# Up projection of 28 expert blocks moved beside the routing and the gate matrix of a PEER layer, activations parked in HBM

## The chip, the cores and the metric

The kernel runs on one core of a Trainium2 chip. The metric is the device time of one execution in microseconds; the time before is the median of three runs.

## What is computed

The reference is one layer of a bidirectional encoder on 512 tokens of width 2048 in fp32: RMSNorm, an input projection, attention in one head group and a gated linear recurrence in the other, an output projection, and then the part that matters here, a PEER channel mixer over 128 x 128 single-neuron experts, and a final RMSNorm. The mixer, cut to its core:

```python
q = (xt @ w_pq).reshape(T, 8, 2, 128)
s1, s2 = q[:, :, 0] @ sub_k1, q[:, :, 1] @ sub_k2      # per head
v1, i1 = top_k(s1, 16);  v2, i2 = top_k(s2, 16)
cand = v1[..., :, None] + v2[..., None, :]             # 256 per head
sc, sel = top_k(cand, 16);  eidx = (i1 * 128 + i2)[sel]
gates = softmax(sc)
out = sum over the 128 chosen e of  gates * gelu(x . u_emb[e]) * v_emb[e]
```

Each token chooses 8 x 16 = 128 of 16384 experts.

## The kernel before

Tokens 160 to 511 (352 of them, TD) are computed densely: all 16384 experts, as 128 blocks of 128 experts, with a gate matrix that is zero where an expert was not chosen. The first 160 tokens are computed sparsely: for each chosen slot a row of u_emb and of v_emb is gathered by an indirect DMA. Both run at the same time in the main loop.

All fp32 products on TensorE are made of three matmuls in a reduced format: an operand is split into `hi` (a cast on ScalarE, L171) and `lo` (raw minus hi, on VectorE, L183), and hi x hi, hi x lo, lo x hi are summed. Weights come in 1 MB tiles, `raw`, two buffers, in the order of a list of sources; `take` splits one tile ahead, and the load of tile i + 2 stands behind the split of tile i on SyncE's queue. So each unit of work on TensorE needs one `hi` on ScalarE and one `lo` on VectorE, made while the unit before it runs.

The stages that the change touches, in order of the program:

1. Projection with w_pq; between its matmuls a hook makes the routing for one set of scores at a time: transposes and scores on TensorE (`route_tr`, `route_sc`), two levels of top 16 on VectorE (`top16`, `route_pair`), and index picking on GpSimd, ScalarE and VectorE (`route_pair`, `route_pick`, `route_sum`).
2. Up blocks 0 to 5 (`u_block`, 48 matmuls, then a gelu on ScalarE, L1046, that leaves the activation `ga` in SBUF); their hooks hold the rest of the routing and the softmax of the gates.
3. The gate matrix, 88 steps of 4 tokens: for each token a product of two one-hot matrices, `ohB` (second key index) and `ohA` (first key index, times the gate), 128 x 128 experts. The one-hots are made in a written-out mix: `ohB` by VectorE alone (L1090), by GpSimd and VectorE (L1073, L1094), or by GpSimd and ScalarE (L1073, L1097, L1099); `ohA` by four VectorE tensor_scalars (L1113) or by VectorE and GpSimd (L1108, L1110). ScalarE copies each step's PSUM into a stage `stg`, which goes to HBM (`gd`) every 8 steps. TensorE does almost nothing else here.
4. Up blocks 6 to 9 with the first weighs. `weigh(b)` multiplies block b's activation with its gates (VectorE, L1202), casts it (ScalarE, `Wh`, L1205) and makes the rest (VectorE, `Wl`, L1206). The gates come from HBM into a single buffer G for four blocks at a time (`load_g`), and the last weigh of four issues the load of the next.
5. The main loop, 16 groups: 8 v units (48 matmuls each: 8 blocks' weighed activations times v) and 8 up blocks for the group after. After each unit `tick` takes 320/230 = 1.39 steps of the gathers: an indirect DMA on GpSimd's queue into one of three buffers, and one pass of VectorE over 2048 elements (`gu`, dot with the token's x, L1242; `gv`, add to the result, L1264). When the list changes from the first 128 tokens to the last 32 (slot list 8), the x tile is loaded anew into its single buffer just before its first use (L1231, L1234). A table W_AT puts the six weighs that aren't done in v units behind the up blocks 1, 2, 4, 5 and 6 of a group, so that the load of G has two units of time between the weigh that issues it and the weigh that needs it.

Engines work each in program order; a waiting instruction holds what stands behind it.

Of the kernel before, what the change touches and what calls it, by code (L numbers as in the profile page):

```python
# [55 lines left out]
def tile_encoder(
# [86 lines left out]
    on_pool = set(range(U_P3 + 2, U_P3 + 9)) | {U_P5, U_P5 + 1, U_P5 + 22}  # L143
    on_both = set(range(U_P5 + 17, U_P5 + 22))
# [717 lines left out]
    ga1p, ga1_close = pool("ga1", bufs=4, side="right")  # L862
# [24 lines left out]
    cur = {}  # L887

# [120 lines left out]

    def hook3(kq, n):  # L1010
        route_hook(kq, n)
        if n == 0:
# [4 lines left out]
    def hook4(kq, n):
        if n == -1:
            route_pair()
            flush_lo()  # L1020
            route_sum()
        elif n == 0:
            softmax_a(2, 4)
        elif n == 1:
            route_pick()
            softmax_b(2)
        else:
            lts[1] = g_lists(1)

    acts = {}  # L1030

    def u_steps(b, hook=None, n=2):
# [12 lines left out]
        ga = p.tile([128, TD], F32, tag="ga", name="ga")
        A.activation(out=ga, in_=ps[:, 0:TD], func=AF.Gelu_apprx_tanh)  # L1046
# [7 lines left out]
    for j, hook in enumerate((route_hook, route_hook, route_hook, hook3, hook4)):
        u_block(j, hook)
    u5 = u_steps(GRP + 1, route_hook, 1)
    next(u5)
    st["defer"] = False
    rt2_close()
    rt1_close()  # L1060
    h0_close()


    oh, oh_close = pool("oh", bufs=2)
    gsp, gs_close = pool("gst", bufs=2)
    NB = 4
    NBB = 6
    A_AHEAD = 3

    def g_diff(lt, ta, mode):  # L1070
        B = oh.tile([128, NB, 128], F32, tag="B", name="ohB", bufs=NBB)
        if mode != "z":
            P.tensor_tensor(B, io_sb.unsqueeze(1).to_broadcast([128, NB, 128]),  # L1073
                            lt[:, 1, ta:ta + NB].unsqueeze(2).to_broadcast([128, NB, 128]), op=ALU.subtract)
# [3 lines left out]
    A_MODE = "tm"  # L1080

    def b_mode(n):
        return B_MODE[n % len(B_MODE)]

    def g_onehot(n):
        B = Bs[n]
        m = b_mode(n)
        if m == "z":
            tm, ta = steps[n]
            V.tensor_tensor(B, io_sb.unsqueeze(1).to_broadcast([128, NB, 128]),  # L1090
                            lts[tm][:, 1, ta:ta + NB].unsqueeze(2).to_broadcast([128, NB, 128]), op=ALU.is_equal)
            flush_evac()
        elif m == "y":
            V.tensor_scalar(out=B, in0=B, scalar1=0.0, scalar2=None, op0=ALU.is_equal)  # L1094
            flush_evac()
        else:
            A.activation(out=B, in_=B, func=AF.Abs)  # L1097
            flush_evac()
            A.activation(out=B, in_=B, func=AF.Relu, scale=-1.0, bias=1.0)  # L1099

    As = {}

    def g_gated(n):
        tm, ta = steps[n]
        lt = lts[tm]
        As[n] = Ao = oh.tile([128, NB, 128], F32, tag="A", name="ohA", bufs=4)
        if A_MODE[n % len(A_MODE)] == "m":
            V.tensor_tensor(Ao, io_sb.unsqueeze(1).to_broadcast([128, NB, 128]),  # L1108
                            lt[:, 0, ta:ta + NB].unsqueeze(2).to_broadcast([128, NB, 128]), op=ALU.is_equal)
            P.tensor_tensor(Ao, Ao, lt[:, 2, ta:ta + NB].unsqueeze(2).to_broadcast([128, NB, 128]), op=ALU.mult)  # L1110
        else:
            for tk in range(ta, ta + NB):
                V.tensor_scalar(out=Ao[:, tk - ta, :], in0=io_sb, scalar1=lt[:, 0, tk:tk + 1],  # L1113
                                scalar2=lt[:, 2, tk:tk + 1], op0=ALU.is_equal, op1=ALU.mult)

    steps = [(tt, t) for tt in range(1, NT) for t in range(NB1 if tt == 1 else 0, 128, NB)]
    Bs = {}
    evac = []

    def flush_evac(keep=1):  # L1120
        while len(evac) > keep:
            stg, o, ps, dst = evac.pop(0)
            A.copy(stg[:, :, o:o + NB], ps.rearrange("p t i -> p i t"))
            if dst is not None:
                A.dma_start(out=dst, in_=stg)

    def g_ahead(n):
        for m in range(n, min(n + NBB, len(steps))):
            if m not in Bs:
                tm, ta = steps[m]  # L1130
                if tm not in lts:
                    lts[tm] = g_lists(tm)
                Bs[m] = g_diff(lts[tm], ta, b_mode(m))

    g_ahead(0)
    for _ in range(KD - 2):
        next(u5)
    for n in range(len(steps)):
        for m in ((0, 1) if n == 0 else (n + 1,)):
            if m < len(steps):  # L1140
                g_onehot(m)
# [4 lines left out]
        B, Ao = Bs.pop(n), As.pop(n)
        o = ((tt - 1) * 128 + ta - NB1) % TB
        if o == 0:
            stg = gsp.tile([128, NBLK, TB], F32, tag="stg", name="stg")
        ps = psA.tile([128, NB, 128], F32, tag="A", name="ps_G")  # L1150
        for t in range(NB):
            T.matmul(ps[:, t, :], B[:, t, :], Ao[:, t, :], start=True, stop=True)  # L1152
        g_ahead(n + 1)
# [345 lines left out]
```

## Time and profile before

| | us |
|---|---|
| median of 3 runs | 3144.4 (3137.42 to 3146.35) |
| the profiled execution | 3137.7 |
| its span, first to last instruction | 3135.8 |
| PE busy | 2955.7 (94%) |
| VectorE (DVE) busy | 2308.8 (74%) |
| ScalarE (ACT) busy | 1138.3 (36%) |
| GpSimd (POOL) busy | 971.4 (31%) |
| mean granted TensorE clock | 0.979 |

The stages that the change touches begin at 875 us, where the first up block starts; the gate matrix lies at 941 to 1117, the first v unit starts at 1157, the last up block at 3049. Shares over the whole span hide this: the stages have different limits. The prediction reads each stage by itself.

### The profile page before, as it was taken

How to read it: one execution, taken by the hardware profiler on the slowest of the kernel's cores; microseconds unless marked ns; L12 is line 12 of the kernel's file. 1: busy time of each engine (PE TensorE's matmuls, PEld its weight loads, DVE VectorE, ACT ScalarE, POOL GpSimd, SP SyncE). 2: the span in 40 equal slices, each digit the busy share in tenths (PEclk: the TensorE clock that was granted, in tenths of full speed). 3: DMA queues.
4: the chain of work that ended last, by engine and by line, in shares of the span. 5: the costliest groups of instructions: out<-in, count | busy, mean ns of one | idle time of the engine just before them, and what ended most of it. 6: DMA issues, size and time to landing. Idle time of an engine off the chain costs nothing. (4 is left out here: it accounts for less than half of the span.)

```text
span 3135.8 us, 41549 instructions
## 1 busy us (share of the span) xinstructions
PE 2955.7 (94%) x16965; PEld 2746.8 (88%) x16965; DVE 2308.8 (74%) x3194; ACT 1138.3 (36%) x1425; POOL 971.4 (31%) x642
## 2 busy tenths in 40 slices
PE   8999999999986679999999999999999989999998
PEld 6777766788886579999999999999999989999997
DVE  6763476446999957778787887787877868878855
ACT  5662344343455533222322323323223222232334
POOL 0000211023666623324333343333333323324302
PEclk9999999999998899999999999999999999999999
DMA  5212311242222358888988988989889878898854
GB/s 222 87 69 98 119 57 41 81 151 88 88 81 108 148 202 335 309 324 314 343 330 317 343 334 323 337 334 334 338 325 341 330 279 336 321 339 323 329 187 158
DMA packets 144783, 746.93 MB, mean 238 GB/s; under 512 B 11984, under 2 KB 57056, under 8 KB 58640
## 3 DMA queue, kind: packets, MB, share of 16 engines
q1 hardware_dynamic: 93792, 368.53, 32.4%
q0 software_dynamic: 48000, 345.73, 29.1%
q10 hardware_dynamic: 2800, 30.02, 2.4%
q8 instruction: 133, 2.18, 0.3%
q14 instruction: 58, 0.48, 0.0%
HBM read 712.51 MB, written 31.72 MB: 237 GB/s over the span
## 5 line engine op out<-in xcount | busy, mean ns | idle before, releaser
L183 DVE TENSOR_TENSOR lo<-raw,hi 128x2048 fp32r<-128x2048 f32 (+1 forms) x306 | 696.0, 2275 | 365.9 <-ACT hi L171 365.8
L171 ACT CAST hi<-raw 128x2048 fp32r<-128x2048 f32 x316 | 602.4, 1907 | 616.4 <-DMA raw<-in_v_t_dram 226.2
L199 PE MATMUL ps_u<-H,hi 128*128 128x352 f32 x2048 | 665.0, 325 | 23.2 <-ACT hi L171 21.7
L201 PE MATMUL ps_u<-H,lo 128*128 128x352 f32 x2048 | 665.4, 325 | 18.4 <-DVE lo L183 17.2
L1306 PE MATMUL ps_v<-Wh,lo 128*128 128x352 f32 x2048 | 662.5, 323 | 18.1 <-DVE lo L183 18.1
L200 PE MATMUL ps_u<-L,hi 128*128 128x352 f32 x2048 | 662.8, 324 | 0.0
L1304 PE MATMUL ps_v<-Wh,hi 128*128 128x352 f32 x2048 | 661.0, 323 | 0.0
L1305 PE MATMUL ps_v<-Wl,hi 128*128 128x352 f32 x2048 | 657.6, 321 | 0.0
L1240 POOL DMA_INDIRECT gu<-in_u_emb_dram,idx x160 | 316.0, 1975 | 626.4 <-DVE x L1264 462.1
L1256 POOL DMA_INDIRECT gv<-in_v_emb_dram,idx x160 | 316.4, 1978 | 606.6 <-DVE gu L1242 464.4
L199 PEld LDWEIGHTS ps_u<-H,hi 128*128 128x128 f32 x2048 | 387.5, 189 | 24.9 <-ACT hi L171 23.1
L201 PEld LDWEIGHTS ps_u<-H,lo 128*128 128x128 f32 x2048 | 387.1, 189 | 25.3 <-DVE lo L183 24.0
L1306 PEld LDWEIGHTS ps_v<-Wh,lo 128*128 128x128 f32 x2048 | 386.1, 189 | 23.7 <-DVE lo L183 23.6
L200 PEld LDWEIGHTS ps_u<-L,hi 128*128 128x128 f32 x2048 | 387.4, 189 | 0.0
L1242 DVE SCALAR_TENSOR_TENSOR gu<-gu,xng 128x2048 f32<-128x2048 f32 x160 | 365.0, 2284 | 29.1 <-DMA xng<-xnd 20.5
L1305 PEld LDWEIGHTS ps_v<-Wl,hi 128*128 128x128 f32 x2048 | 385.7, 188 | 0.0
L1304 PEld LDWEIGHTS ps_v<-Wh,hi 128*128 128x128 f32 x2048 | 384.1, 188 | 1.7 <-issue 1.7
L1264 DVE SCALAR_TENSOR_TENSOR x<-gv,w,x 128x2048 f32<-128x2048 f32 x128 | 300.2, 2345 | 8.0 <-DMA gv<-in_v_emb_dram,idx 8.0
L1316 DVE TENSOR_TENSOR acc<-ps_v,acc 128x352 f32<-128x352 f32 x240 | 123.1, 520 | 135.6 <-PE ps_v L1306 134.4
L1046 ACT ACTIVATE ga<-ps_u 128x352 f32<-128x352 f32 x128 | 59.4, 464 | 449.5 <-PE ps_u L201 449.4
L1205 ACT CAST Wh<-ga 128x352 fp32r<-128x352 f32 x128 | 62.2, 486 | 383.9 <-DVE ga L1202 383.9
L1152 PE MATMUL ps_G<-ohA,ohB 128*128 128x128 f32 x704 | 111.3, 322 | 63.1 <-DVE ohB L1090 42.0
(312 smaller groups left out, 3910.4 us busy)
## 6 DMA issues: line engine op xcount, KB each, us to landing
raw<-in_u_t_dram SPq DMA_DIRECT2D x128, 1024.0 KB, 8.4
raw<-in_v_t_dram SPq DMA_DIRECT2D x128, 1024.0 KB, 7.8
raw<-in_w_dram SPq DMA_DIRECT2D x28, 1024.0 KB, 4.8
gd<-stg ACTq DMA_DIRECT2D x11, 2048.0 KB, 6.7
G<-gd SPq DMA_DIRECT2D x32, 704.0 KB, 9.9
raw<-in_w_out_dram SPq DMA_DIRECT2D x16, 1024.0 KB, 4.8
raw<-in_w_pq_dram SPq DMA_DIRECT2D x16, 1024.0 KB, 4.8
xs<-in_x_dram SPq DMA_DIRECT2D x4, 1024.0 KB, 10.6
```

The lines of the kernel that those rows point to most:

```text
L171: A.copy(hi, raw)
L183: en.tensor_tensor(lo[:, c], raw[:, c], hi.bitcast(F32)[:, c], op=ALU.subtract)
L199: T.matmul(ps, ah, bh, start=first, stop=False)
L200: T.matmul(ps, ah, bl, start=False, stop=False)
L201: T.matmul(ps, al, bh, start=False, stop=last)
L1240: P.indirect_dma_start(out=g, out_offset=None, in_=u_emb, in_offset=bass.IndirectOffsetOnAxis(ap=ix, axis=0))
L1242: V.scalar_tensor_tensor(out=g, in0=g, scalar=1.0, in1=xs_t["x"], op0=ALU.mult, op1=ALU.mult, accum_out=a_t[h][:, k:k + 1])
L1256: P.indirect_dma_start(out=g, out_offset=None, in_=v_emb, in_offset=bass.IndirectOffsetOnAxis(ap=ix, axis=0))
L1264: V.scalar_tensor_tensor(out=d, in0=g, scalar=wk, in1=d, op0=ALU.mult, op1=ALU.add)
L1304: T.matmul(ps[:, 0:TD], hi[:, cc], Wh, start=j == 0, stop=False)
L1305: T.matmul(ps[:, 0:TD], hi[:, cc], Wl, start=False, stop=False)
L1306: T.matmul(ps[:, 0:TD], lo[:, cc], Wh, start=False, stop=j == PR - 1)
```

## The change

- A planner, `stage_plan`, sets at build time what is done between the matmuls of the first 28 up blocks (`hooks`, four places in each block). It walks a list of tasks (the rest of the routing, the softmaxes, the gate matrix steps, `g`, and steps of the gathers, `tick`) with a cost on TensorE, VectorE and ScalarE for each, and places a task where VectorE and ScalarE, by those costs, have caught up with TensorE. It comes to 28 blocks with hooks, and three more before the first v unit (lead0 = 31; before: 10). Blocks 0 to 13 hold the routing, 5 gather steps and the first three pairs of one-hots; blocks 14 to 27 all 88 gate steps and 29 gather steps.
- The one-hots are made without GpSimd: both by a VectorE compare of 128x512 (L1219 of the new kernel), and the gate is multiplied into `ohA` by four ScalarE copies of 128x128 with a scale per partition. They are made three steps ahead in four buffers each.
- The gathers begin beside block 7. In the main loop 286 steps are left, 1.3 a unit.
- The x tile of slot list 8 is requested after the first of six v steps that now stand ahead of its first use.
- 38 activations (blocks 0 to 37) are parked in HBM (`ad`): written on ScalarE's queue behind the gelu, 176 KB each, and read back on SyncE's queue into two buffers (`gr`); the weigh of block b issues the reload of block b + 2.
- Of the main loop's groups the first four have 3 up blocks instead of 8, the fifth 7, the last one before the end 6. In the first four, the six weighs stand in threes behind the first and the second up block.
- The splits that GpSimd had taken over wholly or by half around the routing go to VectorE.

The core of the diff:

```diff
+    tasks += [("pre", m) for m in range(G_AHEAD)]
+    for n in range(len(G_STEPS)):
...
+        tasks += [("g", n)]
...
+        pe += 1.93
+        cur = []
+        while tasks and max(dve, act) <= pe:
+            if ticks_on and since >= 3.5:
+                cur.append(("tick", None))
...
+            if t[0] == "g":
+                cost, arg = (1.36, 1.75, 1.27), t[1]
...
+    for g in range(NP - 1):
+        b0 = (g + 1) * PR
+        r = min(max(3, b0 + PR + LEAD - done), NBLK - done)
...
+            if r >= 7:
+                k = sum(len(W_AT[j]) for j in range(i + 1))
+                now = [b for b in todo if b < b0 + LEAD + k and b < done + i]
+            else:
+                now = [b for b in todo if b < b0 + LEAD + 3 * (i + 1) and b < done + i]
...
-    on_pool = set(range(U_P3 + 2, U_P3 + 9)) | {U_P5, U_P5 + 1, U_P5 + 22}
-    on_both = set(range(U_P5 + 17, U_P5 + 22))
+    on_pool = set(range(U_P3 + 2, U_P3 + 9)) | {U_P5, U_P5 + 1}
+    on_both = set()
...
+    def u_block(b, hook=None):
+        hi, lo = take()
...
+            if hook and k % 4 == 3:
+                hook()
+        ga = uap.tile([128, TD], F32, tag="ga", name="ga")
         A.activation(out=ga, in_=ps[:, 0:TD], func=AF.Gelu_apprx_tanh)
+        if b in ad_at:
+            A.dma_start(out=ad[ad_at[b]], in_=ga)
+        else:
+            acts[b] = ga
...
-        if A_MODE[n % len(A_MODE)] == "m":
-            V.tensor_tensor(Ao, io_sb.unsqueeze(1).to_broadcast([128, NB, 128]),
-                            lt[:, 0, ta:ta + NB].unsqueeze(2).to_broadcast([128, NB, 128]), op=ALU.is_equal)
-            P.tensor_tensor(Ao, Ao, lt[:, 2, ta:ta + NB].unsqueeze(2).to_broadcast([128, NB, 128]), op=ALU.mult)
-        else:
-            for tk in range(ta, ta + NB):
-                V.tensor_scalar(out=Ao[:, tk - ta, :], in0=io_sb, scalar1=lt[:, 0, tk:tk + 1],
-                                scalar2=lt[:, 2, tk:tk + 1], op0=ALU.is_equal, op1=ALU.mult)
...
+    def g_onehots(n):
...
+        for o, j in ((Ao, 0), (B, 1)):
+            V.tensor_tensor(o, io_sb.unsqueeze(1).to_broadcast([128, NB, 128]),
+                            lt[:, j, ta:ta + NB].unsqueeze(2).to_broadcast([128, NB, 128]), op=ALU.is_equal)
+        for t in range(NB):
+            A.activation(out=Ao[:, t, :], in_=Ao[:, t, :], func=AF.Copy, scale=lt[:, 2, ta + t:ta + t + 1])
...
+    def g_step(n):
+        flush_evac()
+        if n + G_AHEAD < len(G_STEPS):
+            g_onehots(n + G_AHEAD)
...
+    def reload():
+        if back:
+            b = back.pop(0)
+            back_t[b] = t = grp.tile([128, TD], F32, tag="gr", name="gr")
+            nc.sync.dma_start(out=t, in_=ad[ad_at[b]])
...
         if j == GRP - 1:
             load_g(b // GRP + 1)
+        if b in ad_at:
+            reload()
...
+    for i, n in enumerate((0, 5, PR + LEAD)):
+        u_block(lead0 - 3 + i)
+        tick()
+        for b in range((0, 0, 5)[i], n):
+            weigh(b)
```

Where instructions move. First, VectorE in the gate matrix, before: the one-hots of about three steps, with nothing between them (`ohA` by compare or by four tensor_scalars, `ohB` by compare).

```order
1040 L1094 TENSOR_SCALAR ohB<-ohB 128x512
1041 L1113 TENSOR_SCALAR ohA<-io_sb,lt 128x128 x4
1042 L1108 TENSOR_TENSOR ohA<-io_sb,lt 128x512
1043 L1090 TENSOR_TENSOR ohB<-io_sb,lt 128x512
1044 L1113 TENSOR_SCALAR ohA<-io_sb,lt 128x128 x4
1045 L1108 TENSOR_TENSOR ohA<-io_sb,lt 128x512
1046 L1090 TENSOR_TENSOR ohB<-io_sb,lt 128x512
1047 L1113 TENSOR_SCALAR ohA<-io_sb,lt 128x128 x4
```

The same engine in one up block of the gate matrix now: `lo` is the split for the next block, `gu` a gather's dot product.

```order
1002 L292 TENSOR_TENSOR lo<-raw,hi 128x2048
1003 L1219 TENSOR_TENSOR ohA<-io_sb,lt 128x512
1004 L1219 TENSOR_TENSOR ohB<-io_sb,lt 128x512
1005 L1219 TENSOR_TENSOR ohA<-io_sb,lt 128x512
1006 L1219 TENSOR_TENSOR ohB<-io_sb,lt 128x512
1007 L1219 TENSOR_TENSOR ohA<-io_sb,lt 128x512
1008 L1219 TENSOR_TENSOR ohB<-io_sb,lt 128x512
1009 L1159 SCALAR_TENSOR_TENSOR gu,act<-gu,xng 128x2048
```

Two such clumps of three pairs and a gather step follow one split; the tensor_scalars are gone, and splits and gather steps have moved in from the main loop.

Second, VectorE behind the up blocks of a main loop group, before: `ga<-ga,G` and `Wl` are a weigh, and G's next load is issued at row 1201.

```order
1197 L1202 TENSOR_TENSOR ga<-ga,G 128x352
1198 L1206 TENSOR_TENSOR Wl<-ga,Wh 128x352
1199 L183 TENSOR_TENSOR lo<-raw,hi 128x2048
1200 L1242 SCALAR_TENSOR_TENSOR gu,act<-gu,xng 128x2048
1201 L1202 TENSOR_TENSOR ga<-ga,G 128x352
1202 L1206 TENSOR_TENSOR Wl<-ga,Wh 128x352
1203 L183 TENSOR_TENSOR lo<-raw,hi 128x2048
1204 L1264 SCALAR_TENSOR_TENSOR x_0_2585<-gv,w,x_0_2585 128x2048
1205 L183 TENSOR_TENSOR lo<-raw,hi 128x2048
1206 L1242 SCALAR_TENSOR_TENSOR gu,act<-gu,xng 128x2048
1207 L1264 SCALAR_TENSOR_TENSOR x_0_2585<-gv,w,x_0_2585 128x2048
1208 L1202 TENSOR_TENSOR ga<-ga,G 128x352
```

And now, behind the first two up blocks of the first group: `gr` is a reloaded activation; the weighs are those of blocks 10, 11, 12, then 13, 14, 15, and G's next load is issued at row 1233.

```order
1231 L1333 TENSOR_TENSOR gr<-gr,G 128x352
1232 L1337 TENSOR_TENSOR Wl<-gr,Wh 128x352
1233 L1333 TENSOR_TENSOR gr<-gr,G 128x352
1234 L1337 TENSOR_TENSOR Wl<-gr,Wh 128x352
1235 L1333 TENSOR_TENSOR gr<-gr,G 128x352
1236 L1337 TENSOR_TENSOR Wl<-gr,Wh 128x352
1237 L292 TENSOR_TENSOR lo<-raw,hi 128x2048
1238 L1181 SCALAR_TENSOR_TENSOR x_0_2586<-gv,w,x_0_2586 128x2048
1239 L1333 TENSOR_TENSOR gr<-gr,G 128x352
1240 L1337 TENSOR_TENSOR Wl<-gr,Wh 128x352
1241 L1333 TENSOR_TENSOR gr<-gr,G 128x352
1242 L1337 TENSOR_TENSOR Wl<-gr,Wh 128x352
```

Between the weigh that issues G's load and the weigh that needs it stood two splits and three gather steps; now they are neighbours.

Third, SyncE's queue at the same place: the transfers of the first group's up blocks and of the next v units now.

```order
23 L266 DMA raw<-in_v_t_dram 128x2048 x5
24 L266 DMA raw<-in_u_t_dram 128x2048 x3
25 L266 DMA raw<-in_v_t_dram 128x2048
26 L1322 DMA gr<-ad 128x352
27 L1327 DMA G<-gd 128x11x128
28 L1322 DMA gr<-ad 128x352 x2
29 L266 DMA raw<-in_v_t_dram 128x2048
30 L1322 DMA gr<-ad 128x352 x2
31 L1327 DMA G<-gd 128x11x128
```

Before, this queue held only raw tiles and G's loads, in the main loop four raw tiles or more between two loads of G; now both loads of G and five reloads lie around one raw tile.

More of the change, by code (lines that the diff above doesn't have):

```diff
@@ L887, in tile_encoder @@
     cur = {}
+    psS = [psB, "B"]
     def route_tr():
@@ L977, in tile_encoder @@
             flush_lo()
-        for tt in order:
+        for tt in order if c == 0 else range(NT):
             q = rt1.tile([128, 512], F32, tag=f"q{tt}", name=f"q{tt}")
@@ L1054, in tile_encoder @@
[L1054 to L1075, printed above, removed]
@@ L1116, in tile_encoder @@
[L1116 to L1133, printed above, removed]
@@ new lines, in flush_evac @@
+    def flush_evac(keep=1):
+        while len(evac) > keep:
+            stg, o, ps, dst = evac.pop(0)
+            A.copy(stg[:, :, o:o + NB], ps.rearrange("p t i -> p i t"))
+            if dst is not None:
+                A.dma_start(out=dst, in_=stg)
+    def g_step(n):
+        flush_evac()
+        if n + G_AHEAD < len(G_STEPS):
+            g_onehots(n + G_AHEAD)
+        tt, ta = G_STEPS[n]
+        B, Ao = Bs.pop(n), As.pop(n)
+        at, o = divmod((tt - 1) * 128 + ta - NB1, TB)
+        if o == 0:
+            gst["stg"] = gst["p"].tile([128, NBLK, TB], F32, tag="stg", name="stg")
+        ps = psA.tile([128, NB, 128], F32, tag="A", name="ps_G")
+        for t in range(NB):
+            T.matmul(ps[:, t, :], B[:, t, :], Ao[:, t, :], start=True, stop=True)
+        evac.append((gst["stg"], o, ps, gd[:, at] if o + NB == TB else None))
@@ new lines, in rep_lists @@
+    def rep_lists():
+        pr = psC.tile([128, 512], F32, tag="C", name="pt_r")
+        T.matmul(pr[:, 0:128], rep1[0:NB1, :], ef[0:NB1], start=True, stop=True)
+        T.matmul(pr[:, 128:256], rep1[0:NB1, :], gts[0:NB1, 1, :], start=True, stop=True)
+        p4 = pr.rearrange("p (a m q) -> p a q m", a=4, q=4)
+        for q in range(4):
+            r = slice(NB1 * q, NB1 * (q + 1))
+            V.tensor_copy(idx1[r], p4[r, 0, q, :])
+            V.tensor_copy(gate1[r], p4[r, 1, q, :])
+    ticks = {"n": 0}
@@ new lines, in tile_encoder, with hook @@
+    st["defer"] = False
+    flush_lo()
+    load(st["split"])
+    load(st["split"] + 1)
+    psS[:] = [psA, "A"]
+    for b in range(lead0 - 3):
+        hk = iter(hooks[4 * b:4 * b + 4])
+        def hook():
+            for name, arg in next(hk):
+                do[name](arg)
+        u_block(b, hook)
+    flush_evac(0)
+    gst["close"]()
+    gst["oh_close"]()
+    lst2_close()
+    accp, _ = pool("acc")
+    wp, _ = pool("w", bufs=PR + LEAD)
+    gp, _ = pool("G", bufs=1)
+    sml, _ = pool("sml", bufs=2)
```

341 lines of the change are left out of this document (172 added, 169 removed).

## The prediction

> **What bounds the kernel now.** I first cut the trace into stretches (the busy time of each engine by windows). The columns are: from:to, length, busy time of PE, PEld, DVE, ACT and POOL with instruction counts, granted clock, DMA share, GB/s.
>
> ```profile
> 875.00:941.00 66.00, 54.91 (x338) 52.62 (x336) 61.39 (x278) 37.24 (x51) 46.18 (x48) 0.97 0.23 81
> 941.00:1118.00 177.00, 114.40 (x725) 105.94 (x726) 172.71 (x288) 92.32 (x166) 110.73 (x99) 0.84 0.31 126
> 1118.00:1157.00 39.00, 31.48 (x185) 30.74 (x184) 15.79 (x20) 12.41 (x15) 1.05 (x2) 0.91 0.72 264
> 1157.00:3049.00 1892.00, 1844.73 (x11423) 1832.56 (x11422) 1473.41 (x1190) 559.07 (x500) 629.50 (x317) 0.99 0.86 321
> ```
>
> The last row is the main loop: TensorE is its bound (1844.7 of 1892 us). The second is the gate matrix: VectorE is the bound (172.7 of 177), TensorE stands idle a third of it and its clock falls to 0.84. So the slack that up blocks can fill lies in 875 to 1157. What the gate matrix consists of is read from the groups by line, for that stretch; the last row is from the groups by line over the whole run.
>
> ```profile
> L1113 DVE TENSOR_SCALAR ohA<-io_sb,lt 128x128 f32<-128x128 f32 x176 | 119.5, 737 | 0.0
> L1152 PE MATMUL ps_G<-ohA,ohB 128*128 128x128 f32 x704 | 111.3, 322 | 63.1 <-DVE ohB L1090 42.0 <-DVE ohB L1094 16.8 <-DVE ohA L1113 3.3
> L1110 POOL TENSOR_TENSOR ohA<-ohA,lt 128x512 f32<-128x512 f32 x44 | 53.5, 1215 | 65.8 <-DVE ohA L1108 65.8
> L1123 ACT COPY stg<-ps_G 128x512 f32<-128x512 f32 x88 | 51.1, 582 | 68.0 <-PE ps_G L1152 67.7
> L1108 DVE TENSOR_TENSOR ohA<-io_sb,lt 128x512 f32<-128x512 f32 x44 | 29.8, 678 | 0.0
> L1090 DVE TENSOR_TENSOR ohB<-io_sb,lt 128x512 f32<-128x512 f32 x34 | 23.1, 678 | 0.0
> ...
> L992 ACT ACTIVATE gts<-gts 128x128 f32<-128x128 f32 x2 | 0.6, 310 | 11.0 <-DVE gts L991 11.0
> ```
>
> TensorE waits for VectorE's one-hots, and VectorE's largest item is L1113, which the change deletes. Durations overlap, so I take costs from the pitch, start to start, in the timeline:
>
> ```profile
> 1036.58 0.68 DVE L1108 TENSOR_TENSOR ohA<-io_sb,lt 128x512 f32<-128x512 f32 x1
> 1037.18 0.68 DVE L1090 TENSOR_TENSOR ohB<-io_sb,lt 128x512 f32<-128x512 f32 x1
> 1037.78 1.06 DVE L1113 TENSOR_SCALAR ohA<-io_sb,lt 128x128 f32<-128x128 f32 x1
> ...
> 1029.67 2.96 PE L1152 MATMUL ps_G<-ohA,ohB 128*128 128x128 f32 x24 [1.67 <-DVE ohB L1090]
> ...
> 1798.46 2.28 DVE L1242 SCALAR_TENSOR_TENSOR gu<-gu,xng 128x2048 f32<-128x2048 f32 x1
> 1800.67 2.28 DVE L183 TENSOR_TENSOR lo<-raw,hi 128x2048 fp32r<-128x2048 f32 x1
> 1802.87 0.51 DVE L1316 TENSOR_TENSOR acc<-ps_v,acc 128x352 f32<-128x352 f32 x1
> ...
> 1252.61 0.47 ACT L1046 ACTIVATE ga<-ps_u 128x352 f32<-128x352 f32 x1 [3.13 <-PE ps_u L201]
> 1252.97 1.90 ACT L171 CAST hi<-raw 128x2048 fp32r<-128x2048 f32 x1
> 1260.29 0.46 ACT L1046 ACTIVATE ga<-ps_u 128x352 f32<-128x352 f32 x1 [5.42 <-PE ps_u L201]
> ```
>
> A one-hot costs VectorE 0.60 us, a gather's sum or a lo split 2.21, a gate step TensorE 2.96/3 = 0.99, and a unit (an up block or a v unit, 48 matmuls) 7.68, from one gelu to the next.
>
> **Part 1: the 28 blocks.** Up to block 13 the hooks hold the rest of the routing, from block 14 on the gate matrix. Two rows of the stretch 870 to 941 give what the routing needs:
>
> ```profile
> L199 PE MATMUL ps_u<-H,hi 128*128 128x352 f32 x95 | 32.2, 339 | 1.5 <-ACT sc L903 1.5
> L183 DVE TENSOR_TENSOR lo<-raw,hi 128x1024 fp32r<-128x1024 f32 x5 | 6.1, 1224 | 0.0
> ```
>
> There, 95/16 = 5.9 blocks took 45.6 of TensorE's 54.9 us, so the routing takes 9; VectorE without its splits 61.4 - 6.1 = 55. Blocks 0 to 13: TensorE 14 x 7.68 + 9 = 116.5; VectorE 55 + 14 splits 31 + 5 gathers 11 + 3 one-hot pairs 4 = 101. TensorE is the bound; with 4 us for waits in order (transposes, lists) 120.
>
> Blocks 14 to 27 carry all 88 gate steps and 29 gathers. VectorE: 176 x 0.60 = 105.6, 14 x 2.21 = 30.9, 29 x 2.21 = 64.1, together 201. TensorE: 14 x 7.68 + 88 x 0.99 = 195. ScalarE: 88 x (0.582 + 4 x 0.310) = 160, plus 14 x (1.90 + 0.47) = 33, together 193; the scaled copy isn't in this trace, and the 0.310 of an activation of the same shape stands for it. GpSimd keeps only the gathers' issues, which hide. Three engines are nearly level, and VectorE leads. Its split must also wait for the hi cast, which ScalarE reaches after the gelu: 0.7 us a block, 10 in all. So 210, bounds 195 (TensorE alone) and 230 (VectorE by durations, 0.678 and 2.29, instead of pitches). The stage: 330 us, from 875 to 1205, call that E; 315 to 360.
>
> **Part 2: the transition.** Three up blocks, ten weighs, then v units. The first gate-matrix loads, the main loop's, and the nearest transfers to the new reloads (176 KB each):
>
> ```profile
> 1131.37 0.61 SPq L1196 DMA_DIRECT2D G<-gd  x1
> ...
> 1138.62 0.53 DVE L1202 TENSOR_TENSOR ga<-ga,G 128x352 f32<-128x352 f32 x1 [9.39 <-DMA G<-gd]
> ...
> 1140.19 0.52 DVE L1202 TENSOR_TENSOR ga<-ga,G 128x352 f32<-128x352 f32 x1
> ...
> 1141.71 0.52 DVE L1202 TENSOR_TENSOR ga<-ga,G 128x352 f32<-128x352 f32 x1
> ...
> DMA to landing us min/median/max: 4.8/9.9/11.3
> ```
>
> ```profile
> gd<-stg ACTq DMA_DIRECT2D x11, 2048.0 KB, 6.7
> xng<-xnd ACTq DMA_DIRECT2D x4, 256.0 KB, 9.3
> xnd<-xn POOLq DMA_DIRECT2D x1, 256.0 KB, 4.2
> ```
>
> A weigh takes 1.51 us. G is a single buffer, loaded by the last weigh of its four (L, 7.2 us at low traffic); a reload is issued two weighs ahead of its use (R; I take 4.2, the smaller of two like transfers, since traffic is low). From E: the gate matrix's last write (6.7) and the first load (7.2) end at 15, as block 29 does. Weighs 0, 1 to 18.9; reload 2 lands 21.6; weighs 2, 3 to 24.6; G lands 30.9; weigh 4, whose Wh stands ahead of the next hi cast on ScalarE, then cast, split: 35.9. A gather, weighs 5, 6 to 41.1, reload 7 at 43.8, weigh 7 at 45.3, G at 51.6, weighs 8, 9, then cast and split of the second v unit: 58.1. It ends 65.8, with the slow clock below 68.5. Five units are 38.4: a loss of 30; 20 if L is 4.8 and no reload is waited for (2 x 2.4 and 2 x 2.7 less), 48 with the longest rows (2 x 4.1 and 2 x 5.1 more).
>
> **Part 3: the first four groups.** Each has 3 up blocks and weighs three blocks at a time, the third always the first of a new G: weighs 10, 11, load, 12. What a VectorE that waits for a transfer does to TensorE is shown once in the trace, at the x tile of slot list 8:
>
> ```profile
> 2544.06 2.29 DVE L1242 SCALAR_TENSOR_TENSOR gu<-gu,xng 128x2048 f32<-128x2048 f32 x1 [11.58 <-DMA xng<-xnd]
> ...
> 2549.54 1.89 ACT L171 CAST hi<-raw 128x2048 fp32r<-128x2048 f32 x1
> 2551.34 0.46 ACT L1046 ACTIVATE ga<-ps_u 128x352 f32<-128x352 f32 x1
> ...
> 2563.19 0.47 ACT L1046 ACTIVATE ga<-ps_u 128x352 f32<-128x352 f32 x1 [4.40 <-PE ps_u L201]
> ...
> 2551.49 0.66 PE L199 MATMUL ps_u<-H,hi 128*128 128x352 f32 x1 [12.14 <-ACT hi L171]
> ...
> 2553.82 0.66 PE L201 MATMUL ps_u<-H,lo 128*128 128x352 f32 x1 [1.37 <-DVE lo L183]
> ```
>
> A wait of 11.6 us cost 12.1 + 1.4 of TensorE idle, and the unit behind it took 11.7 instead of 7.68 + 1.37: 2.65 more, its first matmul 0.66 us long instead of 0.32. That is a low clock after an idle TensorE. In the Trainium skill, "TensorE: Matmul & The Clock Gate", What's actually happening, an idle window of about 3.4 us halves the clock for one more such window. By that an idle stretch costs 1.7, not 2.65, and about nine of them come out 9 us cheaper.
>
> First batch: weighs wait for the gelu of the unit that just ended; weigh 11 releases G 2.2 us into the next unit; after L come 1.0 for product and Wh and 1.9 for the cast. TensorE idles 2.2 + L + 2.9 - 7.68 = L - 2.6, plus 1.4 and 2.65: L + 1.5. Traffic is lighter than in the loop, since the waiting VectorE starts no gathers, and heavier than at the first load, so I take L = 8.5, midway between 7.2 and 9.9: 10 us. Second batch: its third weigh waits for a reload issued after its first; same steps give R + 1.9 = 6.1; the fourth group's blocks 38 and 39 aren't parked: 1.5. Sum 4 x 10 + 3 x 6.1 + 1.5 = 60.
>
> For the reload the Trainium skill gives, in "DMA: Bandwidth & Descriptors", Latency and other measured facts, a fixed cost of about 2 us; with its bandwidth I estimate 2.5 us a reload, and then parts 2 and 3 come out about 8 us lower. No row shows such a transfer.
>
> **Part 4: the rest.** Main loop before: 238 units x 7.68 = 1828 of 1892, so 64 us of losses. 16 of them are the x tile (12.14 + 1.37 + 2.65); now it is requested six v steps before its first use, some 30 us, and this goes. The other 48 over 15 groups are 3.2 each; 11 groups keep the old pattern: 35. Parking the activations is an issue of a DMA on ScalarE's queue behind the gelu, 38 times, hidden. The work before 875 and the tail from 3049 are the same: nothing.
>
> Sum from 875 to the last v group: 330 + 68.5 + 215 units x 7.68 (1651) + 60 + 35 = 2144.5. Before: 66 + 177 + 39 + 1892 = 2174. The change is -29.5 us. The profiled execution took 3137.7, span 3135.8, which is 6.7 below the median of 3144.4; against that median I get 3115.
>
> **The rivals.** *Loads land early* (L 4.8, the shortest row, reloads hidden): first batches 6.3, second 1.4 each, transition 20: 39 us less, 3076. For it: the DMA share was 0.31 at the gate matrix. Against it: raws and gathers are in flight when G is asked for.
>
> *Loads land late* (L 11.3, R 9.3, the longest rows): batches 4 x 12.8 + 3 x 11.2 + 1.5 = 86, transition 48: 44 more, 3159. For it: the loop's DMA share of 0.86, plus 38 writes and reads. The change then does what it says, and all of it is given back.
>
> *The gate matrix runs in lockstep with the blocks.* One-hots are made three steps ahead in four buffers. While TensorE runs three quarters of a block (5.8 us), VectorE can make a split and one step's one-hots, then waits for a buffer. By the pitches it stays busy only if TensorE begins its block 3.3 to 5.6 us ahead of VectorE's split: the pair that VectorE makes 3.4 us after the split's start needs the gate step that TensorE ends 6.7 us into the block, and the block's last gate step, at 12.6, needs the pair that VectorE and ScalarE's four copies end at 7.0. The margin is narrow. If the lead is lost, VectorE's 13.8 us for six steps are lengthened by the 5.8 instead of by the 0.7: 14.7 x 5.1 = 75 us, 3190, slower than before. It decides from 2.7 us a block: (29.5 + 9.4)/14.7. Against it: VectorE has the most work, so TensorE should find itself leading.
>
> **How the numbers follow.** About 0.3%, 9.4 us, is what a measurement of this kernel can tell from no change: faster is below 3135, slower above 3154. Forecast 0.55, its own range 3090 to 3138; early loads 0.20; late loads 0.13, half of it within 0.3%; lockstep 0.12, mostly slower, a partial one less. Faster 0.51 + 0.20 + 0.03 = 0.74, same 0.13, slower 0.13. The range 3070 to 3155 leaves out the lower edge of the early case and the upper halves of the last two.
>
> **What would show it.** Right: blocks 0 to 27 end near 1205; VectorE over 90% busy from block 14 on; TensorE idle of 5 to 10 us, released by the hi cast, twice in each of the first four groups, with VectorE waiting for G and for the reload; no wait for the x tile of list 8. Wrong: TensorE waiting for one-hots or VectorE for gate buffers in every block (lockstep), the stage beyond 1235, G waits under 5 us or over 11, or a new wait in the last groups, where gathers now run to the end.

## The result: 1% slower, and the profile after

The changed kernel took 3173.7 us (median of 4 runs, 3169.4 to 3176.0) beside 3140.9 for the kernel before in the same measurement: ratio 1.0103, 95% interval 1.0079 to 1.0127. Forecast were 3115 us and a gain. The page of the profiled execution (3176.0 us) shows first where it went: total, TensorE's busy share in 40 slices, and its clock.

```profile
span 3174.2 us, 41739 instructions
PE 2967.4 (93%) x16965; PEld 2751.6 (87%) x16965; DVE 2251.3 (71%) x3099; ACT 1199.9 (38%) x1705; POOL 823.8 (26%) x539
...
PE   8999999999997888689888999999999999999998
...
PEclk9999999999998999889899999999999999999999
```

TensorE's row before, 78 us a slice against 79 now:

```profile
PE   8999999999986679999999999999999989999998
```

VectorE and GpSimd have less to do than before, and TensorE's busy time is about the same. Before, TensorE had one deep gap of four slices (12 to 15). Now it is under nine tenths busy, at a clock that dips with it, in all but one of the slices 13 to 22 (950 to 1750 us), and the lowest of them, slice 17, is the transition to the main loop: the gate matrix no longer leaves TensorE idle for long, but a shallow valley reaches far behind it. I cut the trace at the gelus of blocks 13, 27, 31, 43 and 127 (busy time by windows; columns as in the prediction):

```profile
879.00:1030.80 151.80, 125.31 (x737) 122.60 (x736) 100.92 (x317) 63.55 (x81) 43.21 (x48) 0.92 0.47 169
1030.80:1267.60 236.80, 201.65 (x1374) 192.38 (x1374) 199.22 (x234) 176.58 (x458) 49.66 (x29) 0.98 0.78 288
1267.60:1393.80 126.20, 100.45 (x581) 97.81 (x581) 68.79 (x53) 36.55 (x46) 24.10 (x15) 0.89 0.77 283
1393.80:1806.70 412.90, 357.54 (x2114) 351.50 (x2113) 290.03 (x261) 103.00 (x90) 121.33 (x58) 0.92 0.77 282
1806.70:3085.20 1278.50, 1266.83 (x7874) 1260.70 (x7874) 1003.32 (x811) 382.14 (x340) 401.65 (x212) 1.00 0.87 323
```

| stretch | forecast | measured | difference |
|---|---|---|---|
| start to block 0 | 875 | 879 | +4 |
| blocks 0 to 13 (routing) | 120 | 151.8 | +32 |
| blocks 14 to 27 (gate matrix) | 210 | 236.8 | +27 |
| transition: 12 units of 7.68 and a loss of 30 | 122 | 126.2 | +4 |
| first four groups: 44 units and 60 | 398 | 412.9 | +15 |
| the rest: 164 units and 35 | 1295 | 1278.5 | -16 |
| behind the last gelu, as before | 86 | 89.0 | +3 |

These differences, 68 us before rounding, stand between my -29.5 and the measured +38.4 of the spans (3174.2 against 3135.8); 59 of them lie in the stage. (The first row is no finding: block 0's gelu lies between 884 and 892 us in the kernels of this study, and kernels with the same code ahead of it lie up to 6.6 apart.) The odd thing is in the first two rows of the windows. VectorE's work is 100.9 and 199.2 us; I had summed 101 and 201. TensorE's gate half is 201.7; I had 195. (In the routing half TensorE is at 125.3 for my 116.5, at a clock of 0.92.) The work was priced about right, yet no engine is full: 83% and 85% for TensorE, 66% and 84% for VectorE.

Who waits for whom, grouped, first in the routing half (879 to 1031; columns: us in total, times, longest; GpSimd's own waits are left out):

```profile
...
ACT gts L1103 <- DVE gts L1102: 23.9, 3, 15.2
...
PE ps_u L310 <- DVE lo L292: 19.5, 6, 5.8
DVE gu L1159 <- DMA gu<-in_u_emb_dram,idx: 19.3, 2, 10.1
```

The timeline of one of these, by engine:

```profile
949.05 4.13 POOL L1052 TENSOR_TENSOR eq<-ab,io_sb 128x512 f32<-128x512 f32 x2
953.33 1.04 POOL L1157 DMA_INDIRECT gu<-in_u_emb_dram,idx  x1 [0.16 <-issue]
...
962.39 2.29 DVE L1159 SCALAR_TENSOR_TENSOR gu<-gu,xng 128x2048 f32<-128x2048 f32 x1 [10.13 <-DMA gu<-in_u_emb_dram,idx]
...
966.95 0.66 PE L310 MATMUL ps_u<-H,lo 128*128 128x352 f32 x1 [5.79 <-DVE lo L292]
...
974.58 0.31 ACT L1103 ACTIVATE gts<-gts 128x128 f32<-128x128 f32 x1 [15.20 <-DVE gts L1102]
...
976.20 0.46 ACT L1131 ACTIVATE ga<-ps_u 128x352 f32<-128x352 f32 x1
977.06 1.90 ACT L280 CAST hi<-raw 128x2048 fp32r<-128x2048 f32 x1 [0.40 <-ACT ga L1131]
```

The first gather is issued only behind GpSimd's routing work; VectorE stands at its sum for 10.1 us; the next lo stands behind the sum and TensorE waits for it; ScalarE stands at the exp for 15.2 us, with a gelu and a cast behind it. One late transfer holds three queues. In the gate half (1031 to 1268), again without GpSimd's:

```profile
...
ACT ohA L1222 <- DVE ohA L1219: 51.8, 30, 4.7
PEld ps_G L1242 <- ACT stg L1227: 44.4, 43, 3.6
DVE lo L292 <- ACT hi L280: 35.3, 14, 4.3
PE ps_G L1242 <- ACT stg L1227: 19.2, 31, 2.2
```

and one turn of it in the timeline, block 16's end:

```profile
1081.55 1.28 ACT L1222 ACTIVATE ohA<-ohA,lt 128x128 f32<-128x128 f32 x4
1082.73 0.45 ACT L1131 ACTIVATE ga<-ps_u 128x352 f32<-128x352 f32 x1
1083.58 1.90 ACT L280 CAST hi<-raw 128x2048 fp32r<-128x2048 f32 x1 [0.40 <-ACT ga L1131]
...
1085.51 2.29 DVE L292 TENSOR_TENSOR lo<-raw,hi 128x2048 fp32r<-128x2048 f32 x1 [2.58 <-ACT hi L280]
1087.72 0.69 DVE L1219 TENSOR_TENSOR ohA<-io_sb,lt 128x512 f32<-128x512 f32 x1
...
1088.44 1.28 ACT L1222 ACTIVATE ohA<-ohA,lt 128x128 f32<-128x128 f32 x4 [2.47 <-DVE ohA L1219]
...
1090.24 1.16 PE L1242 MATMUL ps_G<-ohA,ohB 128*128 128x128 f32 x8 [1.15 <-DVE ohB L1219]
```

ScalarE's last scaled copies, gelu, hi cast, then VectorE's lo, then its one-hots, then ScalarE's copies again: a ring. VectorE idles while ScalarE casts, ScalarE idles while VectorE splits. For VectorE this one wait, 35.3 us, is nearly all that its 199.2 us of work leave of the 236.8.

### The profile page after: what moved, and what is told of

It is laid out like the page before. It is cut to its first block, busy times and chain, and to the rows that moved or that the text cites. A ratio compares the mean times of both kernels' runs of the same rounds, so it can differ in the third digit from the quotient of the medians.

```text
span 3174.2 us, 41739 instructions
## 1 busy us (share of the span) xinstructions
PE 2967.4 (93%) x16965; PEld 2751.6 (87%) x16965; DVE 2251.3 (71%) x3099; ACT 1199.9 (38%) x1705; POOL 823.8 (26%) x539
## 5 line engine op out<-in xcount | busy, mean ns | idle before, releaser
L292 DVE TENSOR_TENSOR lo<-raw,hi 128x2048 fp32r<-128x2048 f32 x307 | 707.9, 2307 | 404.7 <-ACT hi L280 400.9
L308 PE MATMUL ps_u<-H,hi 128*128 128x352 f32 x2048 | 674.2, 329 | 37.2 <-ACT hi L280 37.2
L1371 PE MATMUL ps_v<-Wh,lo 128*128 128x352 f32 x2048 | 667.4, 326 | 16.2 <-DVE lo L292 16.2
L1370 PE MATMUL ps_v<-Wl,hi 128*128 128x352 f32 x2048 | 665.1, 325 | 0.5
L1173 POOL DMA_INDIRECT gv<-in_v_emb_dram,idx x160 | 305.0, 1906 | 735.5 <-DVE gu L1159 550.2
L1157 POOL DMA_INDIRECT gu<-in_u_emb_dram,idx x160 | 299.7, 1873 | 737.4 <-DVE x L1181 542.2
L1222 ACT ACTIVATE ohA<-ohA,lt 128x128 f32<-128x128 f32 x352 | 112.6, 392 | 56.6 <-DVE ohA L1219 53.7
L1336 ACT CAST Wh<-ga 128x352 fp32r<-128x352 f32 x90 | 43.7, 485 | 237.4 <-DVE ga L1333 237.4
```

The source lines that it names most:

```text
L292: en.tensor_tensor(lo[:, c], raw[:, c], hi.bitcast(F32)[:, c], op=ALU.subtract)
L308: T.matmul(ps, ah, bh, start=first, stop=False)
L1157: P.indirect_dma_start(out=g, out_offset=None, in_=u_emb, in_offset=bass.IndirectOffsetOnAxis(ap=ix, axis=0))
L1173: P.indirect_dma_start(out=g, out_offset=None, in_=v_emb, in_offset=bass.IndirectOffsetOnAxis(ap=ix, axis=0))
L1370: T.matmul(ps[:, 0:TD], hi[:, cc], Wl, start=False, stop=False)
L1371: T.matmul(ps[:, 0:TD], lo[:, cc], Wh, start=False, stop=j == PR - 1)
```

## The experiments

Each is the changed kernel with one edit, unless it says otherwise; "the gate half" is the time from block 13's gelu to block 27's (236.8 us as changed), "the routing half" that from block 0's to block 13's (144.0; the 151.8 of the table count from 879, where block 0 starts). The theories: **A**, VectorE's lo waits in order for the hi cast; **B**, ScalarE's chain of small copies paces the gate steps; **C**, the gathers lengthen the stage; **D**, VectorE has more work than its pitches say.

**e1, lo behind the first one-hots.**

```diff
             for name, arg in next(hk):
                 do[name](arg)
+                if name == "g":
+                    flush_lo()
...
+        st["defer"] = b >= 14
         u_block(b, hook)
+        flush_lo()
+    st["defer"] = False
```

With `defer` set, `take` makes the hi cast and leaves the lo to the next `flush_lo`.

> The changed kernel with VectorE's lo split of the next block moved, in blocks 14 to 27, from the block's start to behind the first pair of one-hots (everything else the same). Theory A (VectorE's queue: the split stands first and waits for ScalarE's hi cast, 14 waits with 35.3 us, and TensorE pays for it later through the one-hots): blocks 14 to 27 fall from 237 us to some 205, the time from 3174 to about 3142. Theory B (ScalarE's chain of a gate step, four scaled copies and one copy out of PSUM at some 1.65 us a step, paces TensorE's gate steps): VectorE's wait goes but the blocks keep 230 us or more, the time stays above 3166. Both theories: blocks 0 to 13 stay at 152.

Measured: 3155.8 us, ratio to the kernel before 1.0062 (1.0041 to 1.0082); gate half 216.8, routing half as it was (142.5). The window of the gate half in e1, and its waits:

```profile
1029.70:1246.50 216.80, 196.36 (x1377) 188.88 (x1376) 197.99 (x232) 176.44 (x456) 55.91 (x28) 1.00 0.83 310
...
ACT ohA L1222 <- DVE ohA L1219: 32.0, 29, 4.0
PEld ps_G L1242 <- ACT stg L1227: 27.9, 38, 2.8
PE ps_G L1242 <- ACT stg L1227: 20.3, 36, 2.7
DVE lo L292 <- ACT hi L280: 16.9, 14, 2.8
```

Moving one instruction a block takes 20 of the 27 us away, and ScalarE's wait for VectorE shrinks with VectorE's for ScalarE, with the same instructions on every engine: A, though 12 us short of its number. The wait for the cast is halved, not gone: with its 16.9 us VectorE's 198.0 again make up nearly the whole stage.

**e2, no scaled copies** (the loop of `A.activation(... scale=lt ...)` deleted, which leaves the gates out of the gate matrix: it measures time alone).

> The changed kernel without the four scaled copies on ScalarE of each gate step: the gates are left out of the gate matrix, 352 small copies fewer, everything else the same. Theory B (ScalarE's chain paces the gate steps): blocks 14 to 27 fall from 237 us to between 195 and 210, where TensorE or VectorE becomes the bound, and the time to some 3140. Theory A (VectorE waits for the hi cast behind the gelu, which ends when the block ends): the cast comes earlier by the copies that stood ahead of it, some 1.3 us a block, and the blocks fall by 20 us at most. A third theory, D (VectorE's work is longer than its pitches, by durations 230 us): no change, 230 or more.

Measured: 3139.5 us in one run; gate half 198.0. Its window:

```profile
1024.60:1222.60 198.00, 193.69 (x1366) 186.61 (x1366) 195.48 (x234) 80.29 (x116) 87.05 (x28) 1.00 0.88 335
```

B's number holds, and A's bound of 20 us fails. With ScalarE light, TensorE and VectorE are both over 97% busy with the work I had summed, which rules out D. A and B are two sides of the ring, and VectorE's wait for the cast shows it: 35.3 us as changed, 16.9 in e1, 2.5 in e2, while the rest of the gate half, 201.5, 199.9 and 195.5 us, hardly moves. e2 alone would not tell the ring from ScalarE's load, since it takes 96 us of ScalarE's work away; e1 takes none.

**e3, the gathers later** (`"tick": lambda _: None` in the stage; the loop takes all 320).

> The changed kernel with the order of everything the same, but none of the 34 gathers in blocks 0 to 27: all of them come in the main loop. Theory C (the gathers are what lengthens the stage: in the routing half their issues stand behind GpSimd's routing work and VectorE waits 19.3 us for two of them, with ScalarE's exp, gelu and cast behind that; in the gate half they are 64 us of VectorE's work): blocks 0 to 13 fall from 152 to 125 to 135, blocks 14 to 27 from 237 to 200 to 210, and since VectorE has room in the main loop (1473 of 1892 us busy before) the time falls by 40 to 55, to about 3125. Theory A and B alone (waits for the hi cast, ScalarE's chain): blocks 0 to 13 fall by the two gather waits at most, 10 to 20 us, blocks 14 to 27 by less than 10, the time to 3150 to 3165.

Measured: 3177.0 us, 1.0135 (1.0107 to 1.0163): no gain, against both. Yet the stage falls by 40: the routing half to 122.1, 22 less, as C has it; the gate half to 219.0, 18 less, between C (200 to 210) and A and B (less than 10 off). The loop from block 43 to the last gelu gives 32 back:

```profile
1775.80:3086.30 1310.50, 1275.07 (x7874) 1262.97 (x7873) 1062.07 (x852) 384.15 (x341) 492.02 (x238) 1.00 0.90 336
```

Against the same 164 units as changed, 1278.5 us, the DMA share is 0.90 instead of 0.87, and ScalarE waits 238 us instead of 176 for raw tiles to land. So "VectorE has room in the loop" was no reason: 26 of the 34 gathers fall in this stretch (GpSimd's x238 against x212), and it pays 1.2 us for each. In the gate half VectorE had 64 us less to do, and the stage fell by 18 only; without the sums VectorE waits longer for the cast, and TensorE, busy 197.5 of the 219.0 us, is the fullest:

```profile
DVE lo L292 <- ACT hi L280: 81.8, 14, 6.2
ACT ohA L1222 <- DVE ohA L1219: 36.0, 16, 3.0
```

**e7, each gather issued a tick ahead of its sum** (`u_step` and `v_step` issue, then do the sum of the step before).

> The changed kernel with every gather issued one tick ahead of its sum (GpSimd's issue of tick n stands ahead of VectorE's sum of tick n-1); number and places of the ticks unchanged. Without the gathers (e3) blocks 0 to 13 had lost 22 us of 144. Theory C1 (a wait in order: the issue stands behind GpSimd's routing work, VectorE waits for the landing, and ScalarE's exp, gelu and cast wait behind it): most of the 22 come back, block 0's gelu to block 13's takes 125 to 130 us instead of 144, the time falls by 15 to about 3159. Theory C2 (it is VectorE's own work, 5 sums of 2.2 us with the routing's 101 us, that is too much there): 138 or more, the time above 3168. Both: the gate half does not change by more than 5 us, since no gather is waited for there.

Measured: 3157.1 us, 1.0073 (1.0052 to 1.0094); routing half 125.9, gate half 235.2. Both as C1 says. The window of the routing half, as changed and in e7:

```profile
886.80:1030.80 144.00, 117.51 (x688) 114.80 (x687) 95.61 (x295) 59.87 (x78) 43.21 (x48) 0.92 0.48 175
...
886.90:1012.80 125.90, 110.77 (x684) 108.32 (x683) 94.33 (x293) 59.92 (x77) 45.86 (x47) 0.97 0.52 192
```

The same work on VectorE, but for 1 us, 18 us sooner done: the five gathers cost waits, not work.

**e8, the gates on GpSimd again.**

```diff
-        for t in range(NB):
-            A.activation(out=Ao[:, t, :], in_=Ao[:, t, :], func=AF.Copy, scale=lt[...])
+        P.tensor_tensor(Ao, Ao, lt[:, 2, ta:ta + NB].unsqueeze(2).to_broadcast([128, NB, 128]), op=ALU.mult)
```

> The changed kernel with the gates multiplied by GpSimd again, one multiplication of 128x512 for a gate step (1.2 us before) instead of ScalarE's four scaled copies; this undoes that part of the change alone. Theory B (ScalarE's chain paces the gate steps; without any multiplication, e2, blocks 14 to 27 took 198 us instead of 237): as e2, 195 to 210, the time about 3140. Rival: GpSimd takes the place of ScalarE: its multiplications slow VectorE's one-hots beside them and the issue of the gathers stands behind them, 220 or more, the time above 3155.

Measured: 3411.8 us, 1.0877 (1.0854 to 1.0901); gate half 460.7. It is on the rival's side (220 or more, above 3155), and far beyond what that had in mind. The waits there:

```profile
...
POOL ohA L1221 <- DVE ohA L1219: 307.0, 86, 14.5
PEld ps_G L1241 <- POOL ohA L1221: 213.9, 81, 13.5
PE ps_G L1241 <- POOL ohA L1221: 191.4, 39, 13.2
DVE gu L1159 <- DMA gu<-in_u_emb_dram,idx: 153.0, 21, 11.3
DVE x L1181 <- DMA gv<-in_v_emb_dram,idx: 59.5, 8, 9.8
```

Two causes were open: a ring through the gather's issue on GpSimd (F), and the multiplications as such (G). Two edits, run once each, tell them apart.

**e13, e8 without gathers in the stage.**

> The gates multiplied by GpSimd (e8) with no gather in blocks 0 to 27 (e3): e8 without the transfers that GpSimd issues. In e8 blocks 14 to 27 took 461 us; VectorE waited 21 and 8 times for a gather to land, 212 us, GpSimd for VectorE's one-hots, TensorE for GpSimd. Theory F (a ring: a gather's issue stands on GpSimd behind multiplications that wait for VectorE's one-hots, and VectorE's next one-hots stand behind the sum that waits for that gather): without gathers blocks 14 to 27 take 225 us at most, about e3's 219. Theory G (GpSimd's multiplications themselves, 1.42 us, and the one-hots that take 1.52 instead of 0.68 us beside them, are too slow): 260 us or more.

**e14, e8 with gathers a tick ahead.**

> The gates multiplied by GpSimd (e8) with every gather issued one tick ahead of its sum (e7). Theory F (the ring through the gather): the issue is out of the ring, so blocks 14 to 27 fall from 461 us to 225 to 260, and blocks 0 to 13 as in e7 from 146 to about 127; the time to 3160 to 3190. Theory G (the multiplications and the slowed one-hots): 400 us or more remain.

Measured: gate half 206.4 in e13 (3171.8 us) and 292.1 in e14 (3211.3). F accounts for the larger part: e14 keeps the gathers and loses 169 of the 461 us, and without gathers (e13) GpSimd is faster than ScalarE's copies (219.0 in e3). But e14 stays 32 us above what F gave. Eleven waits for gathers, 30 us, are left in it, and G has its share: VectorE is busy 259.9 us there for what took 199.2 as changed, and 203.6 in e13 for what took 134.8 in e3. Where that comes from is seen in e13's window and timeline, VectorE's one-hots and then GpSimd's products:

```profile
1008.50:1214.90 206.40, 192.66 (x1367) 187.15 (x1367) 203.59 (x184) 80.17 (x115) 119.30 (x84) 1.00 0.49 186
...
1051.31 0.68 DVE L1219 TENSOR_TENSOR ohB<-io_sb,lt 128x512 f32<-128x512 f32 x1
1051.91 1.53 DVE L1219 TENSOR_TENSOR ohA<-io_sb,lt 128x512 f32<-128x512 f32 x1
1053.36 0.68 DVE L1219 TENSOR_TENSOR ohB<-io_sb,lt 128x512 f32<-128x512 f32 x1
...
1051.46 1.42 POOL L1221 TENSOR_TENSOR ohA<-ohA,lt 128x512 f32<-128x512 f32 x1 [0.63 <-DVE ohA L1219]
```

The compare that begins while GpSimd multiplies takes 1.53 instead of 0.68: it ends 0.56 behind GpSimd's end at 1052.88, as if it had only then begun. The Trainium skill, "SBUF — State Buffer", Who interferes with whom, says that a VectorE instruction with two SBUF inputs contends with a GpSimd instruction that reads SBUF, and that the port pair they share is an exclusive lock; this row, 1.53 instead of 0.68, agrees.

**e5, the gate matrix in pairs** (`GRP = 2`, two G buffers, `load_g(b // GRP + 2)`), **e12, three reload buffers**, and **e6, both.**

> The changed kernel with the gate matrix read in pairs of blocks into two buffers of half the size (same room in SBUF, same bytes), each pair asked for when the pair before the last is weighed, instead of four blocks into one buffer. The stage is the same, 389 us. My prediction's parts 2 and 3 (a weigh that waits for the next G, 10 us in each of the first four groups and two such waits in the transition): the first batches lose 2 instead of 10, the transition some 12 less, the time falls by 40 to 3134. Rival: the reload that is asked for two weighs ahead lands only a little before G did, so the third weigh of a batch waits for that instead: 3 us less a batch, 15 in all, 3160.

> The changed kernel with three reload buffers (and the bf16 junk output that makes room), but the gate matrix in fours in one buffer as changed: the other half of e6. My prediction's part 3 (a batch waits for whichever of gate matrix and reload lands later, and TensorE pays for it): the first batch of each group still waits for the gate matrix (8 to 9 us), the second no longer for its reload, so three times 5 us and a little in the transition go: 3155 to 3160, and neither half alone (this, e5) gives what both together give. Rival: the reloads alone were the loss, and the time is as e6, 3122 to 3130.

> The kernel with the gate matrix in pairs (e5) and, besides, three buffers for the parked activations instead of two, so that a reload is asked for three weighs ahead (the junk output of the final norms becomes bf16 to make room; nothing reads it). In e5, 12 waits of VectorE for a reload with 57.4 us had taken the place of 6 waits for the gate matrix with 44. If these waits are on the path that sets the end, as my prediction's part 3 has it: a batch's third weigh now finds its data, each of the first four groups loses about 4 us instead of the 14 to 22 of e5, the transition some 8 less, and the time falls by 50 us against e5, from 3164 to about 3114. Rival: what is lost around a batch is TensorE's wait for hi and lo behind three weighs in the queues, whatever they wait for, and the landing of a reload (2.2 to 9.0 us) still comes after them: 15 us less at most, 3149.

Measured: e5 3163.7 us, 1.0079 (1.0060 to 1.0097); e12 3153.7, 1.0054 (1.0035 to 1.0074); e6 3122.0, 0.9951 (0.9936 to 0.9966). The loss of the first four groups over 44 units is 75 us as changed, 74 in e5, 60 in e12, 31 in e6. VectorE's waits for the gate matrix and for reloads in these four groups, as changed:

```profile
DVE gr L1333 <- DMA G<-gd: 32.8, 4, 9.1
...
DVE gr L1333 <- DMA gr<-ad: 12.2, 3, 5.5
```

and in e5:

```profile
DVE gr L1333 <- DMA gr<-ad: 40.1, 7, 7.4
```

With the gate matrix there in time the third weigh of a batch (three weighs in a row) waits for its reload instead: the rival of e5. With only the reloads early (e12) the batch still waits for G, 33.6 us. With both, the wait for G is gone and 0.5 us of waits for reloads are left; the loss falls by 44 where the halves gave 1 and 15, and the time comes within 8 us of e6's forecast, far below its rival. The prediction's mechanism for this part, the later of two transfers, is shown. What remains in e6, 31 us, no run takes apart; that it is the cost of three weighs in the queues is a guess.

**e10, the kernel before with the x tile asked for early** (the change's order of slot list 8, nothing else).

> The kernel before with one part of the change alone: the x tile of slot list 8 is asked for six v steps ahead of its first use instead of at it. My prediction's part 4: the wait of 11.6 us there cost TensorE 16.2 us in all, so the time falls by 16 to about 3121. Rival: the loop makes the lost time good elsewhere, since after a stall the raws and gathers are ahead, and the gain is 5 at most.

Measured: 3124.6 us, 0.9964 (0.9953 to 0.9975), 11.3 us less, between the two. In the profiled executions the stretch that holds the wait, block 43's gelu to the last, takes 1285.0 instead of 1299.5 us, 14.5 less, while block 0's gelu comes 6.6 later in e10, in a part that the edit does not touch. So most of the 16.2 comes back where it was lost; that the loop makes a part good is not shown.

**e11, e1 and e6 and e7 together.**

> The changed kernel with the three edits that had helped, together: VectorE's split behind the first one-hots of a block (e1), gathers issued one tick ahead (e7), the gate matrix in pairs with reloads three ahead (e6). If the three losses lie in different stretches, the gains add: 20 us in blocks 14 to 27, 18 in blocks 0 to 13, 52 behind block 27, and the time falls from 3174 to about 3084, 1.7% under the kernel before. Rival: with the gathers issued earlier and the blocks closer together the transfers are denser (DMA share 0.84 in e1's gate half already), and raws or reloads land later: 3105 or more.

Measured: 3086.0 us, ratio 0.9824 (0.9803 to 0.9845), the fastest of all and 2 us from the forecast. The gains add stretch by stretch: routing half 129.0, 15 less than as changed (18 in e7); gate half 215.6, 21 less (20 in e1); the transition and the first four groups 485.6, 54 less (54 in e6). Its TensorE row:

```profile
PE   8999989999999989799999999999999999999998
```

More than four buffers for the one-hots were not tried.

## Why the prediction was wrong, step by step

- **Blocks 0 to 13, the step that failed first:** "TensorE is the bound; with 4 us for waits in order 120." It took 151.8. I had priced five gathers as 11 us of VectorE's work. They were waits: e3, without them, has a routing half of 122.1 instead of 144.0, and e7, with them and issued a tick ahead, 125.9. I counted each gather's sum and not its issue, which the change moved into GpSimd's queue behind the routing. That is 22 of the 32 us; the other 10 stand in e3 as well (129.9 us from block 0's start, TensorE busy 118.4 of them), so the 4 us for waits in order were too few even without gathers, and no run takes these apart.
- **Blocks 14 to 27, the second:** "Its split must also wait for the hi cast, which ScalarE reaches after the gelu: 0.7 us a block, 10 in all. So 210." The step that failed is the 0.7 us a block: the wait was 35.3 us in 14 times, 2.5 each, and these 25 us are nearly all of the 27. The form of my sum held: VectorE's work and its wait for the cast, 199.2 and 35.3, make up the 236.8 but for 2. What I had wrong is why the cast is late. I let it stand behind the gelu alone; ahead of the gelu stand the scaled copies, which wait for VectorE's one-hots (51.8 us in 30 times), and behind the lo stand the next one-hots. So the wait is a turn of a ring through ScalarE and VectorE in program order: e1 shortens it by moving one instruction a block (216.8), e2 by emptying ScalarE's side (198.0). Two of my own signs said the same: VectorE is 84% busy from block 14 on, not over 90%, and block 27 ends at 1268, not before 1235. The sums themselves held.
- **The scaled copy at 0.310** took 0.392 (the row below); the pitch in the runs of four, 1.28 us, is about 0.30. ScalarE's 193 us came out at 176.6, so this did not decide. The Trainium skill, "ScalarE: Activation LUTs", What ACT_TABLE_LOAD costs, has a per-partition scale make an activation dearer; I estimate 0.386 for this shape by its figures, and the row agrees.

```profile
L1222 ACT ACTIVATE ohA<-ohA,lt 128x128 f32<-128x128 f32 x340 | 108.8, 392 | 54.7 <-DVE ohA L1219 51.8 <-DVE ohB L1219 1.6 <-ACT stg L1227 1.2
```

- **The transition** held in its sum, a loss of 34 (126.2 less 12 x 7.68) for 30, in part by luck. The parts were shifted: VectorE waited 8.0 us in two times for G, where I had 12.6, and 13.8 in three times for reloads, where I had 5.4.
- **The first four groups:** the mechanism held (e5, e12, e6): four waits for G of 8.2 us on average, and TensorE idle for the hi cast behind them. From issue to landing a reload, for which I took 4.2 us, takes 2.2 to 9.0 in e5 (5.1 in the median), and G, for which I took 8.5, takes 4.8 to 11.3 in e12 (9.9). The size was 75 for 60. The waits for transfers were worth 44 (e6), near my 49; what I had too small is the loss without any such wait, 31 in e6 where eight batches at 1.4 make 11. Some 5 of that are the loop's steady loss, which I had left out here (an estimate: 19 over 164 units, for 44); the rest stays open.
- **The rest:** the x tile's wait is gone, as forecast, and is worth 11 by the medians and 14.5 in its stretch, for 16 (e10). The steady loss over 164 units is 19 instead of 35. About 10 of these 16 us are my average: the kernel before with the x tile early loses only 25.5 in the same 164 units (e10), where the 48 us over 15 groups gave 35. The other 6 go with the gathers: 216 in this stretch in e10, 212 as changed, 238 in e3, which loses 51. I had not counted that, and it hid a part of the loss in the stage.
- **The rivals.** None of them was this. Lockstep came nearest in place, sign and time (3190), by the wrong ring: VectorE does not wait for gate buffers, it waits for the cast. My argument against it, that VectorE has the most work and so TensorE leads, fails for the ring as well: work of 199 us in 237 leaves room for a wait in every block. "Loads late" has the sign of its part, 15 us of 68.

## What to carry to other kernels

The busy times of a stage bound it from below; when three engines are each busy for about three quarters of it or more and hand work round in program order, follow one turn of the ring before adding a small wait to the largest, and look for the first instruction in a queue that needs another engine's last. A transfer moved into a busy stage is priced by what stands behind its wait in each queue, and issuing it one step ahead of its use may be the whole difference (18 us for five gathers here). Where two transfers feed one step, removing the wait for one shows little until the other is early as well (1 and 15 us here, 44 with both).

## What the runs showed of the hardware

- A VectorE compare of 128x512 takes 0.68 us alone and 1.53 when it begins during a GpSimd multiplication of 128x512 (e13); over the gate half VectorE is then busy 203.6 us instead of 134.8 (e13, e3).
- A gather of 1 MB issued at 953.33 was waited for until 962.39, 9 us, though the DMA share in that stretch, the routing half, was only 0.47.
- 26 more gathers of 1 MB in 164 units of the loop cost 32 us (e3), though VectorE there was busy 78% and the DMA share was 0.87 before they came. TensorE was at 99%.
